# Right factors of the second and third token block made early and loaded at a block's end, and four left factors kept in HBM, in the ConvGLU half of a hybrid trunk kernel

## The chip, the cores and the metric

One core of a Trainium2 chip. The metric is the device time of one execution of the whole kernel in microseconds (us), with the median over the runs shown.

## What is computed

The reference is one layer of a streaming encoder trunk over 2048 frames of width 1024 (float32): an input projection, three token mixers, an output projection with a residual, and a convolutional GLU. The kernel returns the full layer (`out` is 1024 x 2048, transposed). Only the last two steps are touched here:

```
x = x + concat([ya, yb, yc]) @ w_out              # output projection
h = rms_norm(x, ffn_norm_g)
gate, val = split(h @ w_up)                       # w_up: 1024 x 5632
conv = conv_b + sum_i shift(gate, i) * conv_w[i]  # 3 taps along time
x = x + (silu(conv) * val) @ w_down               # w_down: 2816 x 1024
```

## The kernel before

**Precision.** Every matmul operand is a float32 split in a high and a low part (`split`: a cast on ACT, a subtraction on DVE), and every product is made of three matmuls (high x high, high x low, low x high).

**Token blocks.** Output projection and feed-forward go over three blocks of 688, 680 and 680 frames (`BL`), each taken as two halves of n = 344 or 340. In what follows they are the first, second and third block (b = 0, 1, 2 in the code).

**Output projection** (L1179 to L1237). For each block and each half hf it runs 8 k x 8 column tiles ct x 3 matmuls into all 8 PSUM banks. The mixers' output is loaded from HBM (`raw`), split into `yh` (5 buffers) and multiplied by `wo`. Then DVE adds each bank to the residual tile `Y` (L1224; one buffer per ct, loaded from the input for each block), the sum goes to HBM (`x2D`), and its squares are summed. The `stats` of a half (one matmul, Ln and Exp on ACT, giving `rsb`) are run two steps into the next half.

**Right factors.** The up projection uses a Strassen-like scheme: for a column tile fi of 128 of the 2816 hidden columns, 7 products instead of 8. The right factors `B0` to `B6` are made from the normalised block. `build` (L1151) does this in 4 steps j: two normalisations on DVE (L1157), four sums on POOL (L1162 to L1165), seven splits. That is 28 splits of 128 x n a block. The `B` tiles have one buffer each. The first block's factors are built in the output projection, while PE works on the second block's first half. Those of the second and third block are built at the end of the block before, beside the last two down projections (`PACE`).

**Left factors.** For each fi two raw tiles of w_up (512 KB each) are loaded (`up_w`); POOL makes four sums of their quarters (L1268 to L1271), and each of the 7 left factors is split into a `wu` tile (4 buffers) just before its product of 12 matmuls (L1282 to L1284). The products come in the order 0, 1, 6, 2, 3, 4, 5; those numbered 2 to 5 use the sums. All this is repeated for each of the three blocks.

**Down projection.** For each pair of fi, `ffn_down` runs 16 banks x 6 matmuls (L1328 to L1330), and DVE adds each bank to `acc` (L1331). Its weights `wd` are loaded raw and split by ACT and POOL (`down_w`). At a block's end two down projections follow each other, for fi 18, 19 and fi 20, 21. The second pair's weights are asked for after the first of them.

**Order.** The program is written as above, but a list scheduler sets the order on each engine, so rows of an engine can stand far from where they are written. All loads and stores of these stages are issued by one queue, SP, in order; a DMA that waits for a buffer holds up those behind it. The three `raw` buffers serve up and down weights alike.

## Time and profile before

| | |
|---|---|
| time, three runs | 3233.82 us median (3225.78 to 3234.05) |
| profiled execution | 3230.11 us, span 3228.3 us |
| PE busy | 3022.8 us, 94% of the span |
| DVE, ACT, POOL busy | 73%, 43%, 30% |
| output projection of the third block | about 1726.6 to 1787.5 us of the span |
| feed-forward | about 1787.5 to 3224.2 us of the span |

PE is the bound nearly everywhere, so a stretch is read by how many matmuls it starts: the steady feed-forward starts 633 in 100 us with n = 344 and 641 with n = 340, and a stretch that starts fewer has lost the difference. "PEclk" is the clock that TensorE was granted, as a share of 2.4 GHz; 1.00 is full speed and 0.5 would be 1.2 GHz throughout.

### The profile page before, as it was taken

What the parts mean: (1) busy time and instruction counts of PE and PEld (TensorE: products, weight loads), DVE (VectorE), ACT (ScalarE), POOL (GpSimd) and SP (SyncE); (2) the same over time, 40 slices, a digit from 0 to 9 for tenths busy, and PEclk for the clock granted to TensorE, in tenths of its full rate; (3) what the DMA queues carried; (4) which work ended last, traced back from release to release, by engine and by line L of the source; (5) the groups of instructions that cost most, each with busy time, mean ns of one, the idle gap of its engine ahead of it and who ended that gap; (6) DMA issues with size and microseconds to landing.
All of it is one profiled execution on the core that took longest, in us unless ns stands there. A gap on an engine that the chain in (4) does not pass through costs nothing.

```text
span 3228.3 us, 49120 instructions
## 1 busy us (share of the span) xinstructions
PE 3022.8 (94%) x17820; PEld 2638.5 (82%) x17820; DVE 2369.2 (73%) x4590; ACT 1397.6 (43%) x2610; POOL 952.5 (30%) x928
## 2 busy tenths in 40 slices
PE   6988999999999969999989899999899998999999
PEld 4666767777777745667789899998899998899998
DVE  6667676666767546677553788889988889888886
ACT  5434444544543325578532333334333334333332
POOL 1010020001000020144342444444444444444443
PEclk8998999999989979999999999999999999999999
DMA  7756655665634475422234422222422222422221
GB/s 221 210 158 180 200 164 149 182 172 166 173 109 126 141 175 150 127 73 82 77 98 154 134 79 79 77 68 79 157 79 79 79 78 82 134 74 79 79 79 68
DMA packets 310818, 392.92 MB, mean 122 GB/s; under 512 B 137144, under 2 KB 228804, under 8 KB 299752
## 3 DMA queue, kind: packets, MB, share of 16 engines
q1 hardware_dynamic: 305648, 377.99, 39.8%
q0 software_dynamic: 2816, 8.39, 0.9%
q10 hardware_dynamic: 2112, 3.41, 0.5%
q8 instruction: 141, 2.31, 0.3%
q14 instruction: 101, 0.83, 0.1%
HBM read 304.65 MB, written 86.36 MB: 121 GB/s over the span
## 4 chain that ended last, share of the span: by engine, by line
PE 66%; DVE 18%; issue 5%; DMA 4%; ACT 4%; POOL 2%; SPq 0%; POOLq 0%; ACTq 0%; DVEq 0%
PE ps L1284 7%; PE ps L1283 7%; PE ps L1282 7%; PE ps L1330 4%; PE ps L1328 4%; PE ps L1329 4%; PE mm L263 3%; PE mm L261 3%; PE mm L262 3%; PE o L1054 2%; DVE T L516 2%; DVE tm L513 2%; PE z L632 1%; PE ps L1190 1%; PE ps L1189 1%
## 5 line engine op out<-in xcount | busy, mean ns | idle before, releaser
L1284 PE MATMUL ps<-B,wu 128*128 128x340 f32 (+1 forms) x1848 | 593.4, 321 | 20.6 <-DVE wu L143 20.5
L1282 PE MATMUL ps<-B,wu 128*128 128x340 f32 (+1 forms) x1848 | 589.3, 319 | 3.5 <-ACT wu L142 2.4
L1283 PE MATMUL ps<-B,wu 128*128 128x340 f32 (+1 forms) x1848 | 591.8, 320 | 0.0
L1284 PEld LDWEIGHTS ps<-B,wu 128*128 128x128 f32 x1848 | 348.0, 188 | 28.1 <-DVE wu L143 27.7
L1328 PE MATMUL ps<-hid,wd 128*128 128x340 f32 (+1 forms) x1056 | 341.5, 323 | 14.3 <-ACT wd L142 10.2
L1282 PEld LDWEIGHTS ps<-B,wu 128*128 128x128 f32 x1848 | 347.9, 188 | 4.5 <-ACT wu L142 2.7
L1283 PEld LDWEIGHTS ps<-B,wu 128*128 128x128 f32 x1848 | 348.5, 189 | 0.3 <-DVE B L143 0.2
L1330 PE MATMUL ps<-hid,wd 128*128 128x340 f32 (+1 forms) x1056 | 339.6, 323 | 4.4 <-POOL wd L143 4.4
L1329 PE MATMUL ps<-hid,wd 128*128 128x340 f32 (+1 forms) x1056 | 339.6, 322 | 0.0
L261 PE MATMUL mm<-hT,w 128*128 128x512 f32 x704 | 312.6, 444 | 23.7 <-ACT w L142 15.3
L143 DVE TENSOR_TENSOR wu<-S,wu 128x512 fp32r<-128x512 f32 x264 | 256.2, 975 | 75.6 <-ACT wu L142 75.5
L262 PE MATMUL mm<-hT,w 128*128 128x512 f32 x704 | 289.6, 411 | 6.2 <-DVE hT L143 5.9
L263 PE MATMUL mm<-hT,w 128*128 128x512 f32 x704 | 289.4, 411 | 3.9 <-DVE w L143 3.8
L1331 DVE TENSOR_TENSOR acc<-acc,ps 128x340 f32<-128x340 f32 (+1 forms) x528 | 248.7, 505 | 52.8 <-PE ps L1330 51.6
L143 POOL TENSOR_TENSOR wd<-raw,wd 128x1024 fp32r<-128x1024 f32 x66 | 170.7, 2610 | 277.5 <-ACT wd L142 272.5
L142 ACT CAST wu<-S 128x512 fp32r<-128x512 f32 x264 | 163.1, 619 | 151.1 <-PE ps L1284 142.1
L1328 PEld LDWEIGHTS ps<-hid,wd 128*128 128x128 f32 x1056 | 201.2, 191 | 18.0 <-ACT wd L142 11.0
L143 DVE TENSOR_TENSOR wu<-raw,wu 128x512 fp32r<-128x512 f32 x198 | 203.3, 1028 | 5.6 <-ACT wu L142 5.6
L1330 PEld LDWEIGHTS ps<-hid,wd 128*128 128x128 f32 x1056 | 200.1, 190 | 6.6 <-POOL wd L143 6.6
L1329 PEld LDWEIGHTS ps<-hid,wd 128*128 128x128 f32 x1056 | 200.7, 190 | 0.0
L261 PEld LDWEIGHTS mm<-hT,w 128*128 128x128 f32 x704 | 137.8, 196 | 67.5 <-ACT w L142 16.7
L142 ACT CAST wu<-raw 128x512 fp32r<-128x512 f32 x198 | 121.5, 620 | 164.2 <-PE ps L1284 139.7
(335 smaller groups left out, 6816.4 us busy)
## 6 DMA issues: line engine op xcount, KB each, us to landing
w<-wD SPq DMA_DIRECT2D x72, 1024.0 KB
raw<-in_w_up_dram SPq DMA_DIRECT2D x132, 512.0 KB
raw<-in_w_down_dram SPq DMA_DIRECT2D x66, 512.0 KB
wD<-w SPq DMA_DIRECT2D x24, 1024.0 KB
wraw<-in_w_in_dram SPq DMA_DIRECT2D x24, 512.0 KB
xt<-in_xT_dram SPq DMA_DIRECT2D x48, 256.0 KB
K<-qkD SPq DMA_DIRECT2D x21, 512.0 KB
Q<-qkD SPq DMA_DIRECT2D x84, 128.0 KB
```

Source lines behind the costliest of these rows:

```text
L142: (hi_eng or nc.scalar).copy(hi, src) if (hi_eng or nc.scalar) is nc.scalar else hi_eng.tensor_copy(out=hi, in_=src)
L143: (lo_eng or nc.vector).tensor_tensor(lo, src, f(hi), op=ALU.subtract)
L261: mm(ps, hi[:, kt, 0:P], hT[kt][:, 0, :], start=(kt == 0), stop=False)
L262: mm(ps, hi[:, kt, 0:P], hT[kt][:, 1, :], start=False, stop=False)
L263: mm(ps, lo[:, kt, 0:P], hT[kt][:, 0, :], start=False, stop=(kt == KT - 1))
L1282: mm(ps, whl[:, 0, kt, :], Bs[p][:, kt, 0, 0:n], start=(kt == 0), stop=False)
L1283: mm(ps, whl[:, 0, kt, :], Bs[p][:, kt, 1, 0:n], start=False, stop=False)
L1284: mm(ps, whl[:, 1, kt, :], Bs[p][:, kt, 0, 0:n], start=False, stop=(kt == 3))
L1328: mm(ps, wd[:, 0, ch], hid[:, 0, cs], start=(u == 0), stop=False)
L1329: mm(ps, wd[:, 0, ch], hid[:, 1, cs], start=False, stop=False)
L1330: mm(ps, wd[:, 1, ch], hid[:, 0, cs], start=False, stop=(u == G - 1))
L1331: nc.vector.tensor_tensor(acc[ct][:, cs], acc[ct][:, cs], ps, op=ALU.add)
```

## The change

The names in the new code: `put(p, j, o)` is called for each of the 28 splits of a build. `direct` splits into the `B` tile as before; `stored` splits into a small `st` tile (two buffers) and writes it to HBM (`BD`).

- The second block's right factors are built and stored in the output projection, in the third block's first half.
- The third block's are built by `build_ahead(2)`, written in the second block's loop, and stored.
- At a block's end the 7 `B` tiles are loaded (1.4 MB each).
- In the first block, for fi > 1, each `wu` tile of the products 2 to 5 is also written to HBM (`kept`, 80 stores of 512 KB). The second and third block load them (160 loads) instead of making sums and splits, and load only half of the second raw tile.
- The last two down weights of a block are split ahead into four `wu` tiles (`down_last`). `wu` has 5 buffers instead of 4.
- The scratch for software DMA descriptors is cut from 8192 to 2048.

```
-    def build(Bs, b, src, tmp):
+    def build(put, b, src, tmp):
...
-                split(Bs[p][:, j, 0, 0:n], Bs[p][:, j, 1, 0:n], o)
+                put(p, j, o)
                 yield
...
+    def direct(Bs, n):
+        return lambda p, j, o: split(Bs[p][:, j, 0, 0:n], Bs[p][:, j, 1, 0:n], o)
+    later = {}
+    def stored(b):
+        n = BL[b][1]
+        later[b] = [dram.tile([P, 4, 2, n], F32, name=f"BD{b}{p}") for p in range(7)]
+        def put(p, j, o):
+            t = st4.tile([P, 2, HN], F32R, name="st")
+            split(t[:, 0, 0:n], t[:, 1, 0:n], o)
+            nc.sync.dma_start(out=later[b][p][:, j], in_=f(t[:, :, 0:n]))
+        return put
...
-                    if b == 1 and hf == 0:
-                        Bs = factors()
-                        work = build(Bs, 0, lambda kt, done=done: done[kt], tmp3)
+                    if hf == 0:
+                        if b == 1:
+                            Bs = factors()
+                        put = direct(Bs, BL[0][1]) if b == 1 else stored(1)
+                        work = build(put, b - 1, lambda kt, done=done: done[kt], tmp3)
...
+            k0 = 4 * part if (fi, 2) in kept and b else 0
+            nc.sync.dma_start(out=raw[:, k0:KT], in_=w_up[fi, part][:, k0:KT])
...
+            if left[p] is None:
+                nc.sync.dma_start(out=f(whl), in_=kept[fi, p])
+            else:
+                split(whl[:, 0], whl[:, 1], left[p])
+            if b == 0 and fi > 1 and 2 <= p <= 5:
+                kept[fi, p] = dram.tile([P, 2, 4, P], F32, name=f"wuD{fi}_{p}")
+                nc.sync.dma_start(out=kept[fi, p], in_=f(whl))
...
-        ready, work = [], iter(())
+        ready, work = [], build_ahead(2) if b == 1 else iter(())
...
+            for _ in itertools.islice(work, 2 if fi > 2 else 0):
+                pass
...
+        wdl = down_last(range(NF - G, NF))
         if b + 1 < len(BL):
...
             Bs = factors()
-            work = build(Bs, b + 1, load, tmp4)
+            for p in (0, 1, 6, 2, 3, 4, 5):
+                nc.sync.dma_start(out=f(Bs[p][:, :, :, 0 : BL[b + 1][1]]), in_=later[b + 1][p])
```

**DVE, third block's output projection.** The first fence is before: the last two `yh` splits of the first half, then the eight additions of its banks to Y0 to Y7, then the second half's splits.

```order
L143 TENSOR_TENSOR yh_16554<-raw_16552,yh_16554 128x340
L143 TENSOR_TENSOR yh_16591<-raw_16589,yh_16591 128x340
L1224 TENSOR_TENSOR Y0_16465<-Y0_16465,ps_16221 128x340
L1224 TENSOR_TENSOR Y1_16466<-Y1_16466,ps_16222 128x340
L1224 TENSOR_TENSOR Y2_16467<-Y2_16467,ps_16223 128x340
L1224 TENSOR_TENSOR Y3_16468<-Y3_16468,ps_16224 128x340
L1224 TENSOR_TENSOR Y4_16469<-Y4_16469,ps_16225 128x340
L1224 TENSOR_TENSOR Y5_16470<-Y5_16470,ps_16226 128x340
L1224 TENSOR_TENSOR Y6_16471<-Y6_16471,ps_16227 128x340
L1224 TENSOR_TENSOR Y7_16472<-Y7_16472,ps_16284 128x340
L143 TENSOR_TENSOR yh_16620<-raw_16618,yh_16620 128x340
L143 TENSOR_TENSOR yh_16649<-raw_16647,yh_16649 128x340
```

The second is the same engine in the changed kernel, at the end of the same stretch. `st` rows are splits of the second block's right factors.

```order
L143 TENSOR_TENSOR st_16527<-tmp_16440,st_16527 128x340
L143 TENSOR_TENSOR st_16541<-Y3_15891,st_16541 128x340
L1244 TENSOR_TENSOR Y6_16633<-Y6_16633,ps_16230 128x340
L143 TENSOR_TENSOR st_16545<-Y7_15895,st_16545 128x340
L143 TENSOR_TENSOR st_16549<-tmp_16534,st_16549 128x340
L1244 TENSOR_TENSOR Y3_16630<-Y3_16630,ps_16227 128x340
L143 TENSOR_TENSOR st_16553<-tmp_16535,st_16553 128x340
L143 TENSOR_TENSOR st_16586<-tmp_16533,st_16586 128x340
L143 TENSOR_TENSOR st_16590<-Y7_15895,st_16590 128x340
L143 TENSOR_TENSOR st_16594<-tmp_16536,st_16594 128x340
L1244 TENSOR_TENSOR Y7_16634<-Y7_16634,ps_16287 128x340
L143 TENSOR_TENSOR yh_16840<-raw_16838,yh_16840 128x340
```

The additions that free the first half's banks now stand among the 28 `st` splits: Y0 behind the ninth, Y7 behind the last.

**SP, first feed-forward block.** In the changed kernel these rows are from fi = 2 and 3 of the first block: `BD2x<-st` are stores of the third block's right factors, `wuD` stores of left factors, `raw<-in_w_up` the loads of coming weights.

```order
L1187 DMA BD22_21982<-st_22844 128x2x340
L1302 DMA raw_17764<-in_w_up_dram 128x1024
L1325 DMA wuD3_2_17679<-wu_17676 128x1024
L1325 DMA wuD3_3_17698<-wu_17695 128x1024
L1187 DMA BD23_21983<-st_22848 128x2x340
L1187 DMA BD24_21984<-st_23125 128x2x340
L1187 DMA BD25_21985<-st_23129 128x2x340
L1288 DMA x4_24130<-x2D_73 128x680
L1187 DMA BD26_21986<-st_23268 128x2x340
L1302 DMA raw_17766<-in_w_up_dram 128x1024
L1302 DMA raw_17919<-in_w_up_dram 128x1024
```

The scheduler has moved the whole third-block build, which is written in the second block's loop, into the first seven fi of the first block. Its 28 stores and its `x4` loads stand among the weights' loads.

**SP, end of the first block.** Before, from the raw tiles of the next block's fi = 1 (the two `in_w_up` rows) to the last load of `acc` (some rows of the same kind are not shown):

```order
L1264 DMA raw_21892<-in_w_up_dram 128x1024
L1264 DMA raw_21894<-in_w_up_dram 128x1024
L1316 DMA raw_21904<-in_w_down_dram 128x1024
L1374 DMA out_0_dram<-acc0_16830 128x688
L1374 DMA out_0_dram<-acc1_16831 128x688
L1374 DMA out_0_dram<-acc2_16832 128x688
L1339 DMA acc0_21741<-x2D_73 128x680
L1339 DMA acc1_21742<-x2D_73 128x680
L1374 DMA out_0_dram<-acc3_16833 128x688
L1374 DMA out_0_dram<-acc7_16837 128x688
L1339 DMA acc7_21748<-x2D_73 128x680
```

After, from the first `B` load (likewise):

```order
L1419 DMA B0_21686<-BD10_16294 128x8x340
L1419 DMA B1_21687<-BD11_16295 128x8x340
L1419 DMA B6_21692<-BD16_16300 128x8x340
L1419 DMA B5_21691<-BD15_16299 128x8x340
L1426 DMA out_0_dram<-acc0_16992 128x688
L1426 DMA out_0_dram<-acc7_16999 128x688
L1398 DMA acc0_21964<-x2D_73 128x680
L1398 DMA acc7_21971<-x2D_73 128x680
L1302 DMA raw_22122<-in_w_up_dram 128x1024
L1302 DMA raw_22124<-in_w_up_dram 128x1024
L1302 DMA raw_22279<-in_w_up_dram 128x1024
L1302 DMA raw_22281<-in_w_up_dram 128x512
```

The two raw tiles of the next block's fi = 1 stood ahead of the stores of `out` and the loads of `acc`; now they stand behind all sixteen.

## Rows read from the trace of the kernel before

**Rows 1.** The page: the span, PE's busy time, the clock granted in 40 slices, and two of the costliest groups (busy us, mean ns of one, idle time before them and its releaser).
```profile
span 3228.3 us, 49120 instructions
PE 3022.8 (94%) x17820; PEld 2638.5 (82%) x17820; DVE 2369.2 (73%) x4590; ACT 1397.6 (43%) x2610; POOL 952.5 (30%) x928
PEclk8998999999989979999999999999999999999999
L1284 PE MATMUL ps<-B,wu 128*128 128x340 f32 (+1 forms) x1848 | 593.4, 321 | 20.6 <-DVE wu L143 20.5
L1328 PE MATMUL ps<-hid,wd 128*128 128x340 f32 (+1 forms) x1056 | 341.5, 323 | 14.3 <-ACT wd L142 10.2
```

**Rows 2.** Stretches of the feed-forward. Columns: from and to, length; busy us of PE with the instructions started, the same for its weight loads, DVE, ACT, POOL; granted clock; DMA share; GB/s. Steady, end of the first block, steady, end of the second block, end of the kernel.
```profile
core 0: us, PE busy (x) PEld busy (x) DVE busy (x) ACT busy (x) POOL busy (x), PEclk, DMA share, GB/s
2000.00:2100.00 100.00, 100.00 (x633) 100.00 (x632) 87.29 (x128) 39.02 (x58) 45.16 (x35) 1.00 0.23 76
2200.00:2350.00 150.00, 133.35 (x797) 127.07 (x797) 139.66 (x193) 59.81 (x101) 74.38 (x59) 0.98 0.37 121
2400.00:2500.00 100.00, 100.00 (x641) 100.00 (x640) 88.12 (x128) 38.69 (x58) 43.97 (x35) 1.00 0.23 77
2700.00:2800.00 100.00, 85.74 (x502) 80.38 (x501) 93.36 (x132) 40.63 (x72) 52.14 (x43) 0.95 0.43 137
3200.00:3226.00 26.00, 21.32 (x124) 20.20 (x122) 10.73 (x22) 1.99 (x2) 4.70 (x2) 0.93 0.26 100
```

**Rows 3.** What PE waited for in the stretches 2200 to 2350 and 2700 to 2800: us in total, times, longest.
```profile
PE ps L1284 <- DVE wu L143: 7.5, 8, 2.6
PE ps L1328 <- ACT wd L142: 4.7, 1, 4.7
...
PE ps L1284 <- DVE wu L143: 6.5, 9, 1.2
PE ps L1328 <- ACT wd L142: 4.8, 1, 4.8
```

**Rows 4.** The build at the first block's end, 2200 to 2350: minimum, median and maximum ns of one split's halves on ACT and DVE, and of a normalisation on DVE.
```profile
L142 ACT CAST B<-u x16: 474/477/479, 2234.8 to 2277.7; 128x340 fp32r<-128x340 f32 x16
L143 DVE TENSOR_TENSOR B<-u,B x16: 500/598/2255, 2237.8 to 2282.4; 128x340 fp32r<-128x340 f32 x16
L1157 DVE SCALAR_TENSOR_TENSOR x<-x,pps,rsb x8: 914/920/1959, 2249.9 to 2306.9; 128x680 f32<-128x680 f32 x8
```

**Rows 5.** Output projection of the third block: the stretch (columns as in rows 2), the end of the statistics of the half before it on ACT, and the first additions of PSUM banks, of the half before it and of its first half, on DVE.
```profile
1725.00:1795.00 70.00, 70.00 (x448) 69.34 (x448) 25.27 (x46) 19.80 (x42) 21.24 (x21) 1.00 0.44 140
1737.44 0.49 ACT L1235 ACTIVATE rsb<-rsb 128x340 f32<-128x340 f32 x1
1726.56 3.73 DVE L1224 TENSOR_TENSOR Y<-Y,ps 128x340 f32<-128x340 f32 x8 [3.15 <-PE ps L1191]
1756.98 3.33 DVE L1224 TENSOR_TENSOR Y<-Y,ps 128x340 f32<-128x340 f32 x7 [3.17 <-PE ps L1191]
```

**Rows 6.** The first block's build in the output projection: the stretch, the end of the statistics and the first split's cast on ACT, then ns of one of the splits' halves and of one POOL sum.
```profile
1660.00:1710.00 50.00, 39.20 (x224) 37.41 (x223) 37.73 (x54) 22.38 (x50) 26.51 (x23) 0.90 0.39 113
1661.67 0.49 ACT L1235 ACTIVATE rsb<-rsb 128x344 f32<-128x344 f32 x1
1663.58 0.48 ACT L142 CAST B<-Y 128x344 fp32r<-128x344 f32 x1 [0.17 <-DVE Y L1157]
L142 ACT CAST B<-tmp x16: 477/479/483, 1665.6 to 1692.7; 128x344 fp32r<-128x344 f32 x16
L143 DVE TENSOR_TENSOR B<-tmp,B x16: 502/671/1241, 1667.4 to 1693.9; 128x344 fp32r<-128x344 f32 x16
L1163 POOL TENSOR_TENSOR tmp<-tmp,Y x4: 919/1250/1437, 1665.7 to 1689.3; 128x344 f32<-128x344 f32 x4
```

**Rows 7.** DMA times: two kinds of store from the POOL queue (KB each, us from issue to landing); the last store of the kernel, 340 KB, as SP issues it, and SP's wait for it after that; a 512 KB load as SP issues it (first of three) and the POOL sum that waits for it.
```profile
yD<-yl POOLq DMA_DIRECT2D x16, 256.0 KB, 3.7
yD<-yo POOLq DMA_DIRECT2D x32, 128.0 KB, 2.3
3224.78 0.33 SPq L1374 DMA_DIRECT2D out_dram<-acc  x1
SPq L1453 <- DMA out_dram<-acc: 1.8, 1, 1.8
1986.19 10.35 SPq L1264 DMA_DIRECT2D raw<-in_w_up_dram  x3
1989.76 1.61 POOL L1268 TENSOR_TENSOR S<-raw 128x512 f32<-128x512 f32 x1 [0.79 <-DMA raw<-in_w_up_dram]
```

**Rows 8.** The busiest stretch of the DMA engines in the output projection (columns as in rows 2).
```profile
1735.00:1745.00 10.00, 10.00 (x64) 9.67 (x63) 1.50 (x3) 2.46 (x5) 0.33 (x1) 1.00 0.98 337
```

**Rows 9.** The start of the feed-forward: the stretch, what PE waited for, and an ACT row that waits for a raw weight.
```profile
1787.50:1860.00 72.50, 64.10 (x388) 62.18 (x388) 61.27 (x89) 30.62 (x51) 32.73 (x24) 0.98 0.45 146
PE ps L1284 <- DVE wu L143: 6.0, 5, 1.8
PE ps L1282 <- ACT wu L142: 2.4, 1, 2.4
1797.97 1.05 ACT L142 CAST wd<-raw 128x1024 fp32r<-128x1024 f32 x1 [5.52 <-DMA raw<-in_w_down_dram]
```

**Rows 10.** Left factors in the first block's steady part, 1860 to 2200 (ns of one, minimum, median, maximum), and two POOL rows that stand one pair of fi apart.
```profile
L142 ACT CAST wu<-S x67: 602/621/627, 1859.9 to 2198.0; 128x512 fp32r<-128x512 f32 x67
L143 DVE TENSOR_TENSOR wu<-S,wu x67: 678/692/1942, 1860.5 to 2198.7; 128x512 fp32r<-128x512 f32 x67
1983.76 5.22 POOL L143 TENSOR_TENSOR wd<-raw,wd 128x1024 fp32r<-128x1024 f32 x2 [9.30 <-ACT wd L142]
2025.59 5.22 POOL L143 TENSOR_TENSOR wd<-raw,wd 128x1024 fp32r<-128x1024 f32 x2 [9.30 <-ACT wd L142]
```

**Rows 11.** What PE waited for in the kernel's last 25 us.
```profile
PE ps L1330 <- POOL wd L143: 2.2, 2, 1.1
PE ps L1328 <- ACT wd L142: 0.7, 1, 0.7
```

More of the change, by code (lines that the diff above doesn't have):

```diff
@@ L1263, in up_w @@
             raw = raw4([P, KT, P])
-            nc.sync.dma_start(out=raw, in_=w_up[fi, part])
+            k0 = 4 * part if (fi, 2) in kept and b else 0
+            nc.sync.dma_start(out=raw[:, k0:KT], in_=w_up[fi, part][:, k0:KT])
             raws.append(raw)
+        if b and (fi, 2) in kept:
+            return raws[0][:, 0:4], raws[0][:, 4:8], None, None, None, None, raws[1][:, 4:8]
         (a11, a12), (a21, a22) = ((r[:, 0:4], r[:, 4:8]) for r in raws)
@@ L1318, in down_w, with down_last @@
         split(wd[:, 0], wd[:, 1], raw, None, nc.gpsimd)
-        return wd
+        return lambda s, ct: wd[:, s, ct * P : (ct + 1) * P]
+    def down_last(fis):
+        raws = []
+        for fi in fis:
+            raw = raw4([P, DM])
+            nc.sync.dma_start(out=raw, in_=w_down[fi * P : (fi + 1) * P, :])
+            raws.append(raw)
+        whl = [[ws4.tile([P, 2, 4, P], F32R, name="wu") for _ in fis] for h in range(2)]
+        for u, raw in enumerate(raws):
+            for h in range(2):
+                t = whl[h][u]
+                split(t[:, 0], t[:, 1], raw[:, h * 512 : h * 512 + 512].rearrange("p (a c) -> p a c", c=P), None, nc.gpsimd)
+        return [lambda s, ct, u=u: whl[ct // 4][u][:, s, ct % 4, :] for u in range(len(fis))]
     def ffn_down(acc, grp, n):
         for ct in range(KT):
-            ch = slice(ct * P, (ct + 1) * P)
             for hf in range(2):
```

45 lines of the change are left out of this document (23 added, 22 removed).

## The prediction

> **What bounds the kernel now.** I read the page first: PE is busy for 3022.8 of 3228.3 us, and its clock is granted in full in nearly every slice of the feed-forward [rows 1]. Then I counted matmuls by stretch. The steady feed-forward starts 633 or 641 matmuls in 100 us, with PE at 100.00 [rows 2], which is 0.158 or 0.156 us each. There only PE's own work counts, and relief for DVE, ACT or POOL is worth nothing. The time that can be had lies where PE starts fewer:
> - End of the first block, 2200 to 2350: 797 matmuls, where about 955 would fit (150 us at the mean of the two rates). 158 x 0.157 = 24.8 us are lost [rows 2].
> - End of the second block, 2700 to 2800: 502 where 641 would fit. 139 x 0.156 = 21.7 us are lost [rows 2].
> - End of the kernel: the last 26 us hold 124. PE's work ends some 2 us before the stretch does, so 24.2 us could hold 155, and 31 x 0.156 = 4.8 us are lost [rows 2].
> - Start of the feed-forward, 1787.5 to 1860: 388 where 459 would fit at the first rate. 71 x 0.158 = 11.2 us are lost [rows 9, 2].
>
> The waits at the block ends say what it is: PE waits for left-factor splits on DVE (7.5 and 6.5 us) and for the down weights' cast on ACT (4.7 and 4.8 us) [rows 3], while DVE is busy for 139.66 of 150 us [rows 2]. What the waits do not explain is the clock, 0.98 and 0.95 there [rows 2].
>
> **The sum, term by term.** It is made against the profiled execution, 3230.1 us, which lies 3.7 under the median of the runs.
>
> *Block ends.* The 28 splits, 8 normalisations and 16 POOL sums go [rows 4], and the last down weights are split earlier, so both named waits lose their cause: 24.8 + 21.7 = 46.5 us can come back. In their place 7 x 1.39 = 9.75 MB of factors are loaded for each block. At 337 GB/s, the rate of the busiest stretch of the projection [rows 8], that is 29 us. The loads can start when the last up projection has used B0. Six of its products and two down projections are left, 6 x 12 + 2 x 96 = 264 matmuls, 41 us, which hide them. What may be late is the raw pair for fi = 1, which now stands behind 8 stores and 8 loads of 340 KB. The stores of out end with the last down projection; 2.8 MB of acc loads at 337 GB/s take 8.3 us after it, and 1 MB of raw 3.1 us, with about 2 us of latency. That is 13 us into the next block, and its second up projection starts 7 x 12 x 0.156 = 13.1 us into it, with a split of 1.3 us ahead of it [rows 10]. So between 0 and 6 us are lost at each of two ends. I take 1.5 each: **-43.5** (-46 to -35).
>
> *End of the kernel.* The waits there are for the last down weights [rows 11], which are now split beside the down projection before: **-4.3** (-4.8 to 0).
>
> *Output projection of the third block.* This is the price. Call s the start of the bank additions of the half before, 1726.6. Now the third block's first half ends at s + 30.4 (1756.98), and the second at s + 61 [rows 5]. PE has no gap there, DVE is busy for 25 of 70 us [rows 5], so the work has room. But the 28 splits go through two st tiles, and the additions that free the banks stand among them on DVE, the last behind the 28th. The second half needs these banks. The statistics are ready at s + 11.4 [rows 5], and in the first block's build the first split follows 1.4 us behind them [rows 6]: s + 12.8. An st tile is taken for a cast (0.48), a subtraction (0.5 to 0.67, rows beside it in [rows 6]), some 0.2 of hand-over, and the store. Two tiles overlap, so the interval is x = (1.25 + store) / 2. The trace has no such store from SP. Nearest: the last store of out, same size, 0.33 us of issue and 1.8 of wait, 2.1 us on an idle queue; 256 KB from POOL's queue takes 3.7 [rows 7]. That gives x between 1.68 and 2.48 us. I take 1.8, near the store of the same size and queue, a little longer because Y loads share the SP queue, and the next Y load waits for POOL to be done with the old Y. The last split ends at s + 12.8 + 27 x 1.8 + 1 = s + 62.4. Behind it come 2 us of addition and statistics, 15 matmuls of the last bank and the 72 of k = 5 to 7 (yh has five tiles, so they wait), 87 x 0.157 = 13.7 us: s + 78 to 80, against s + 61. With 2 us of lower clock, as in the stretch of the first block's build (0.90) [rows 6]: **+21**. Each 0.1 us of x is worth 2.7 us. The ends are +18 (x = 1.68) and +39 (x = 2.48). If the stores cost nothing, the splits go at the pace of that first build, 1.1 us each [rows 6], the last ends at s + 44, and the loss is 0 to 2.
>
> The Trainium skill ("DMA: Bandwidth & Descriptors", section "Anatomy of one DMA — SWDGE (gpsimd) path") gives about 2.0 us fixed plus bytes at 436 GB/s for a DMA, most of the fixed part being the receipt of the write, heaviest in HBM. It is written for another queue than SP's; by it 340 KB would take 2.8 us as an estimate, x would be 2.03, this term +27 and the whole sum 6 us worse. The row of the same size says 2.1 us [rows 7], and I stay with the row.
>
> *Start of the feed-forward.* The third block's build, 28 splits, 8 normalisations and 16 sums, falls into the first seven fi. One fi is half of 41.83 us [rows 10], so there are 146 us, of which DVE has 13 to 18% free [rows 2], 19 to 26 us. It gets 28 x 0.55 + 8 x 0.92 = 23 us [rows 4]. In the mean it fits; in bursts it won't, and a left-factor split on DVE can take 1.9 us instead of 0.69 [rows 10]. I charge 10 us. Against it, the second half of the projection is late, so the first raw tiles are there in time, and of the 11.2 us lost now (8.4 in waits for first left factors, with ACT held 5.5 us by a raw down weight) [rows 9] I give back 4. Net **+6** (-5 to +20).
>
> *Steady blocks.* 80 stores and 160 loads of 512 KB, 42 and 84 MB, lie beside a queue that moves 76 GB/s [rows 2] and has shown 337 [rows 8]. A 512 KB load takes 3.6 us from issue to use [rows 7], and a wu tile is free for more than that in a ring of five products of 1.9 us each. The sums and splits saved have no price, since PE is full. **+1** (0 to +10). The smaller descriptor scratch and the fifth wu buffer: 0.
>
> Sum: -43.5 - 4.3 + 21 + 6 + 1 = -19.8, so 3210 from the profiled execution and 3214 from the median. Forecast: **3212 us**.
>
> **Rivals.**
> 1. *The price is dearer, the gain is eaten.* A store as slow as the POOL queue's 3.7 us gives +39 instead of +21 [rows 7]; or the start costs its upper end, +20, because SP holds stores of st behind loads that wait for a raw buffer, and ACT then waits for an st tile with left factors behind it. Either leaves -2 to -6: 3224 to 3240. For it: st has two tiles. Against: the same-size store takes 2.1.
> 2. *Slower.* The same st ring, with one mechanism: a store lands late because the Y load ahead of it on SP waits for POOL. The other terms give -40.8, so the balance is at x = 2.53 us, and it is slower by more than 9.7 us from x = 2.9, a store that lands 4.5 us after its split. At 5 us x is 3.1 and the time 3245. Against: only 8 of 28 stores have a Y load ahead of them.
> 3. *The stores are hidden.* If landing takes 1 us or less, or the additions get by earlier, the projection costs 2 instead of 21 and the time is about 3193. Against: the shortest store that the trace shows is 2.1 us [rows 7].
> 4. *The block ends don't come back,* because the loads of B are late. At half of 337 GB/s they would take 58 us against 41 and give back 15 of 22 us at each end: about 3240. Against: the other traffic there is some 76 GB/s [rows 2].
>
> **How the numbers follow.** A change under 0.3% (9.7 us) can't be told from none. The forecast's case, 3201 to 3224, has 0.50; rival 1, with rival 4 in its reach, 0.23; rival 2 0.14; rival 3 0.13. So faster 0.63, same 0.23, slower 0.14. The range takes in most of rivals 1 and 3: 3194 to 3243.
>
> **What would show it.** At both block ends matmuls at 64 in 10 us, DVE well under full, no wait for ACT wd. In the third block's projection a stretch in which PE stands for some 15 to 20 us, waiting for DVE's additions to Y, with `st` casts on ACT waiting for DMA, 1.7 to 2.0 us apart. In the first seven fi a few waits for DVE or ACT wu. I am wrong if st splits are over 2.5 us apart, if PE still waits at the block ends (for B, acc or raw), or if the steady blocks drop under 640 in 100 us in the loads of wu.

## The result: 37 us slower

The changed kernel takes 3270.61 us (median of 4 runs, 3254.61 to 3278.11) against 3233.48 us before (median of 4 runs, one more than the three above): 1.0114 times as long (95% interval 1.0072 to 1.0155). The forecast was 3212 us with a range up to 3243, so it missed in size and in sign. The profiled execution is the fastest of the four, 3254.6 us with a span of 3252.7 us, 24.4 us above the span before.

PE takes the same matmuls in nearly the same order in both kernels. So the time of a stage can be read from the starts of its first matmul and of the next stage's. This table is worked out from these starts in the two traces, in us. The feed-forward has 8712 matmuls, 2904 a block. The first 1848 of a block are as many as seven pairs of fi have, each with its two up projections and one down projection.

```
stage (in matmuls)                        before   after   change   forecast
up to the third block's projection        1729.6  1729.3    -0.3
third block's projection                    61.0   102.5   +41.5      +21
feed-forward, first block: first 1848      304.4   323.2   +18.8       +6
    its last 1056                          182.4   167.3   -15.1  |
second block: first 264                     51.0    49.4    -1.6  |  -43.5
    its last 2640                          428.4   413.2   -15.2  |
third block: first 264                      48.9    50.5    +1.6  |
    its last 2640, to the end              422.5   417.2    -5.3       -4.3
```

The gain at the block ends is there, though smaller than forecast: 30.3 us. Two prices, 41.5 and 18.8 us, eat it twice over. The forecast sum was -19.8 (with +1 for the steady blocks, which has no row here), the measured one is +24.4. Of these 44 us the projection makes 20.5, the start of the feed-forward 12.8, and the block ends with the starts of the blocks behind them 13.2.

The page after, as [rows 1]: the span, the engines, and one of PE's groups with the idle time ahead of it.

```profile
span 3252.7 us, 49359 instructions
PE 3028.6 (93%) x17820; PEld 2647.1 (81%) x17820; DVE 2159.4 (66%) x4430; ACT 1305.7 (40%) x2456; POOL 701.4 (22%) x774
...
L1387 PE MATMUL ps<-hid,wd 128*128 128x340 f32 (+1 forms) x960 | 307.8, 321 | 3.6 <-DVE acc L1390 2.4
```

PE's wait for `ACT wd`, 10.2 us at L1328 before, is gone from the same matmuls after (L1387). PE now waits elsewhere. Stretches after, as [rows 2, 5, 9] (matmuls in brackets after PE's busy time, then the other engines; at the end the granted clock, DMA share and GB/s):

```profile
1750.00:1775.00 25.00, 19.13 (x111) 18.32 (x109) 11.26 (x22) 7.44 (x16) 6.83 (x7) 0.93 0.84 247
1775.00:1800.00 25.00, 12.73 (x48) 11.59 (x49) 7.75 (x14) 6.47 (x14) 5.19 (x7) 0.65 0.77 220
1800.00:1825.00 25.00, 15.48 (x68) 14.20 (x67) 5.40 (x10) 7.28 (x15) 5.86 (x8) 0.67 0.45 150
1850.00:2000.00 150.00, 130.32 (x763) 124.95 (x762) 133.61 (x189) 60.02 (x102) 75.72 (x59) 0.95 0.64 221
2000.00:2100.00 100.00, 100.00 (x633) 100.00 (x632) 83.07 (x129) 40.38 (x61) 52.46 (x34) 1.00 0.54 184
2300.00:2400.00 100.00, 94.32 (x588) 93.05 (x587) 67.55 (x110) 27.84 (x42) 21.33 (x18) 0.98 0.68 245
2750.00:2850.00 100.00, 94.57 (x584) 93.08 (x583) 71.24 (x112) 27.34 (x42) 20.64 (x19) 0.97 0.69 241
3226.00:3252.00 26.00, 22.90 (x147) 22.62 (x146) 13.20 (x27) 0.00 (x0) 0.00 (x0) 1.00 0.28 108
```

Three stretches of 25 us in the projection start 111, 48 and 68 matmuls where about 160 fit. From 1850 to 2000, in the first block's early fi, 763 start where 950 fit. The steady rate is back at 2000 (633). The two stretches with a block's end and the start of the next have 588 and 584 where 641 fit.

What PE waited for in the projection, from 1735 to 1830, and what ACT waited for (us in total, times, longest):

```profile
PE ps L1207 <- DVE Y L1244: 18.1, 6, 9.0
PE ps L1253 <- POOL rsb L1249: 8.9, 1, 8.9
...
ACT st L142 <- DMA BD<-st: 34.7, 20, 3.0
```

ACT's casts into `st` wait 34.7 us for earlier stores to land. PE waits for the additions to Y, which stand behind these splits, and at the end of the stretch 8.9 us for the statistics. The chain of work that ended last in this stretch names the stores (start, us from issue to landing):

```profile
1759.77 3.91 DMA BD<-st
...
1778.80 4.93 DMA BD<-st
...
1801.82 2.66 DMA BD<-st
```

Eight such pieces between 1758 and 1804 have a mean of 3.55 us. The 28 splits on DVE start between 1739.40 and 1806.23: 2.48 us apart in the mean.

In the first fi of the feed-forward, from 1850 to 2000 (PE, then ACT):

```profile
PE ps L1330 <- DVE wu L143: 11.0, 7, 2.6
...
ACT st L142 <- DMA BD<-st: 55.1, 18, 7.1
```

DVE's time for the 28 splits and 8 normalisations of a build (busy us, mean ns of one), first where the changed kernel runs the third block's, 1850 to 2010, then in the kernel before, at the first block's end, 2200 to 2350:

```profile
L143 DVE TENSOR_TENSOR st<-t,st 128x340 fp32r<-128x340 f32 x16 | 15.8, 986 | 5.5 <-ACT st L142 5.4
L143 DVE TENSOR_TENSOR st<-x,st 128x340 fp32r<-128x340 f32 x12 | 9.8, 817 | 4.3 <-ACT st L142 4.3
L1158 DVE SCALAR_TENSOR_TENSOR x<-x,pps,rsb 128x680 f32<-128x680 f32 x8 | 11.1, 1390 | 1.3 <-DMA x<-x2D 1.2
...
L143 DVE TENSOR_TENSOR B<-u,B 128x340 fp32r<-128x340 f32 x16 | 11.9, 748 | 2.7 <-ACT B L142 2.7
L143 DVE TENSOR_TENSOR B<-x,B 128x340 fp32r<-128x340 f32 x12 | 12.8, 1073 | 0.0
L1157 DVE SCALAR_TENSOR_TENSOR x<-x,pps,rsb 128x680 f32<-128x680 f32 x8 | 9.3, 1178 | 0.0
```

That is 36.7 us after and 34.0 before, where the forecast has 23.

And at the first block's end: PE's waits between 2290 and 2420, SP's issues in order (start, us in all, count), and the first cast of the next block's fi = 1:

```profile
PE ps L1328 <- ACT wu L142: 3.0, 1, 3.0
PE ps L1330 <- DVE wu L143: 2.2, 2, 1.4
...
2294.89 16.19 SPq L1419 DMA_DIRECT2D B<-BD  x6
2311.18 12.27 SPq L1426 DMA_DIRECT2D out_dram<-acc  x8
2323.50 6.13 SPq L1398 DMA_DIRECT2D acc<-x2D  x8
2329.99 1.72 SPq L1302 DMA_DIRECT2D raw<-in_w_up_dram  x2
...
2337.97 1.89 ACT L142 CAST wu<-raw 128x512 fp32r<-128x512 f32 x3 [0.74 <-DMA raw<-in_w_up_dram]
```

B, out, acc and the raw pair come in the order that the changed kernel's schedule gave them. The pair is issued between 2329.99 and 2331.7, and ACT gets the first tile at 2337.97, 8 us after its issue, behind 2.8 MB of acc loads and 15.6 us into the second block.

### The profile page after: what moved, and what is told of

Same layout as the page of the kernel before. It is cut to its first block, busy times and chain, and to the rows that moved or that the text cites. A ratio compares the mean times of both kernels' runs of the same rounds, so it can differ in the third digit from the quotient of the medians.

```text
span 3252.7 us, 49359 instructions
## 1 busy us (share of the span) xinstructions
PE 3028.6 (93%) x17820; PEld 2647.1 (81%) x17820; DVE 2159.4 (66%) x4430; ACT 1305.7 (40%) x2456; POOL 701.4 (22%) x774
## 4 chain that ended last, share of the span: by engine, by line
PE 67%; DVE 15%; DMA 7%; ACT 4%; issue 4%; POOL 2%; SPq 0%; ACTq 0%; DVEq 0%; POOLq 0%
PE ps L1329 8%; PE ps L1330 8%; PE ps L1328 8%; PE ps L1387 5%; PE ps L1388 5%; PE ps L1389 5%; PE mm L263 3%; PE mm L261 3%; PE mm L262 3%; PE o L1054 2%; DMA BD<-st 2%; DVE T L516 2%; DVE tm L513 2%; PE z L632 2%; PE st L1036 1%
## 5 line engine op out<-in xcount | busy, mean ns | idle before, releaser
L1328 PE MATMUL ps<-B,wu 128*128 128x340 f32 (+1 forms) x1848 | 592.8, 321 | 10.7 <-ACT wu L142 9.0
L1328 PEld LDWEIGHTS ps<-B,wu 128*128 128x128 f32 x1848 | 350.3, 190 | 12.8 <-ACT wu L142 10.5
L1390 DVE TENSOR_TENSOR acc<-acc,ps 128x340 f32<-128x340 f32 (+1 forms) x528 | 256.6, 505 | 108.6 <-PE ps L1389 108.6
L1387 PE MATMUL ps<-hid,wd 128*128 128x340 f32 (+1 forms) x960 | 307.8, 321 | 3.6 <-DVE acc L1390 2.4
L1388 PE MATMUL ps<-hid,wd 128*128 128x340 f32 (+1 forms) x960 | 306.7, 319 | 1.2 <-DVE hid L143 1.2
L1389 PE MATMUL ps<-hid,wd 128*128 128x340 f32 (+1 forms) x960 | 306.7, 319 | 0.0
L143 POOL TENSOR_TENSOR wd<-raw,wd 128x1024 fp32r<-128x1024 f32 x60 | 148.7, 2499 | 289.1 <-ACT wd L142 288.5
L143 DVE TENSOR_TENSOR wu<-raw,wu 128x512 fp32r<-128x512 f32 x198 | 163.9, 830 | 48.0 <-ACT wu L142 42.6
L261 PEld LDWEIGHTS mm<-hT,w 128*128 128x128 f32 x704 | 138.4, 197 | 66.5 <-ACT w L142 16.9
L1387 PEld LDWEIGHTS ps<-hid,wd 128*128 128x128 f32 x960 | 181.1, 189 | 5.7 <-DVE acc L1390 3.6
L1388 PEld LDWEIGHTS ps<-hid,wd 128*128 128x128 f32 x960 | 180.5, 188 | 1.5 <-DVE hid L143 1.5
L1389 PEld LDWEIGHTS ps<-hid,wd 128*128 128x128 f32 x960 | 180.6, 188 | 0.0
L262 PEld LDWEIGHTS mm<-hT,w 128*128 128x128 f32 x704 | 138.3, 196 | 45.4 <-issue 10.3
L263 PEld LDWEIGHTS mm<-hT,w 128*128 128x128 f32 x704 | 137.8, 196 | 37.8 <-DVE w L143 6.9
```

What stands on the lines that cost most here:

```text
L143: (lo_eng or nc.vector).tensor_tensor(lo, src, f(hi), op=ALU.subtract)
L261: mm(ps, hi[:, kt, 0:P], hT[kt][:, 0, :], start=(kt == 0), stop=False)
L262: mm(ps, hi[:, kt, 0:P], hT[kt][:, 1, :], start=False, stop=False)
L263: mm(ps, lo[:, kt, 0:P], hT[kt][:, 0, :], start=False, stop=(kt == KT - 1))
L1328: mm(ps, whl[:, 0, kt, :], Bs[p][:, kt, 0, 0:n], start=(kt == 0), stop=False)
L1387: mm(ps, wd(0, ct), hid[:, 0, cs], start=(u == 0), stop=False)
```

## The experiments

Each is compared with runs of the kernel before on the same chip, whose medians were 3236.3 to 3236.4 us. Stage times are those of each kernel's own profile, by the method of the table above. Where the code is the same, a stage differs mostly by under 1 us between profiles, but the projection with its stores has 102.5 to 106.6 us and the first 1848 matmuls beside the third block's build 323.2 to 326.6. The start of the third block's projection differs by up to 14 us between profiles of kernels that are the same up to there, so stages are compared, not spans.

**1. One piece for each partition in st.**

```
-            t = st4.tile([P, 2, HN], F32R, name="st")
+            t = st4.tile([P, 2 * HN], F32R, name="st")[:, 0 : 2 * n].rearrange("p (s c) -> p s c", s=2)
```

> The changed kernel, with one edit: the st tile holds its two parts side by side, so that each partition's 2720 bytes are one piece in SBUF as they are in HBM (before: two pieces of 1360). Theory A (a store lands 3.7 us after its split because it is cut into twice as many pieces as the 340 KB store of out, which took 2.1 us): the ACT casts into st come about 1.7 to 1.8 us apart instead of 2.48, the third block's projection is some 18 us shorter, and the start of the feed-forward some us. Theory B (the stores are late because of the other traffic in the queue or the writing itself): casts 2.4 to 2.5 us apart, time within 5 us of the changed kernel.

Measured: 1.0097 (1.0065 to 1.0128). Splits 2.28 us apart, the projection 96.8 us (102.5 in the changed kernel), the first 1848 matmuls 324.8. The size of the pieces is worth some 6 us, a third of what theory A asked for. B is nearer.

**2. Five st tiles in the projection.**

```
+    def stored(b, ring=(None,)):
+        ring = itertools.cycle(ring)
...
+            pool = next(ring) or st4
+            t = pool.tile([P, 2, HN], F32R, name="st", bufs=2 if pool is st4 else 3)
...
-                        put = direct(Bs, BL[0][1]) if b == 1 else stored(1)
+                        put = direct(Bs, BL[0][1]) if b == 1 else stored(1, (st4, y3, y3, st4, y3))
```

> The changed kernel, with five st tiles instead of two in the third block's projection alone (two as before in the feed-forward). Theory A (what costs is the latency of a store, seen through a ring of two): the splits run at the pace of the direct build, 1.1 to 1.3 us apart, the projection gives back 30 to 38 of the 40 us that it lost, about 3235 us. Theory B (what costs is the DMA rate: 28 stores, the Y loads, the mixers' output and x2D are about 18 MB, 54 us at 337 GB/s): the splits come 1.7 to 2.0 us apart and 10 to 20 us come back. The start of the feed-forward stays as it is, some 29 us of PE lost between 1850 and 2000, by both.

Measured: 1.0063 (1.0039 to 1.0086). The splits come 1.33 us apart, as theory A said: latency through a ring of two set the pace, since the same DMA engines move a store every 1.33 us when five may be under way. But theory A's time did not come: the projection still takes 96.8 us. SP's rows (start, us, count) and PE's longest wait say why:

```profile
1750.66 32.30 SPq L1189 DMA_DIRECT2D BD<-st  x27
1783.05 4.50 SPq L1242 DMA_DIRECT2D Y<-in_xT_dram  x7
1788.36 6.84 SPq L1247 DMA_DIRECT2D x2D<-Y  x8
1795.25 9.14 SPq L1216 DMA_DIRECT2D raw<-yD  x8
...
PE ps L1209 <- ACT yh L142: 29.1, 1, 29.1
```

SP now issues 27 stores in a row, then seven Y loads, then the stores of x2D, then the second half's inputs, and PE stands for 29.1 us until the first of those is split. The Y tiles have one buffer, so the additions that free the banks can't run before the build has read the old Y. The ring was one link of the chain, and this order is the next.

**3. Third block's factors built at the second block's end, as before the change.**

```
-        ready, work = [], build_ahead(2) if b == 1 else iter(())
+        ready, work = [], iter(())
...
+            if b + 1 == 2:
...
+                work = build(direct(Bs, n1), b + 1, load, tmp4)
```

> The changed kernel, but the third block's right factors are built at the second block's end straight into the B tiles, as before the change; the rest stays. Theory A (the third block's build, moved by the scheduler into the first fi of the first block, costs some 18 us there because ACT stands waiting for st tiles with the left factors' casts behind it): the start loses about 11 us instead of 29, as before, and the second block's end loses about 20 instead of 9: net 5 to 10 us faster than the changed kernel. Theory B (the start suffers from the stores of left factors and the late end of the projection, not from that build): the start stays at 25 to 30 us and the kernel gets about 10 us slower.

Measured: 1.0059 (1.0038 to 1.0079). The first 1848 matmuls take 301.0 us instead of 323.2, and the second block's last 2640 take 420.9 instead of 413.2. The build costs 22 us where the scheduler put it, and saves 8 where it was taken from. (The projection, the same code as in the changed kernel, took 106.6 us here against 102.5.) The stores of left factors cost nothing here: experiment 12, which has none, also takes 301.0 for the first 1848.

**4. Both builds inside the running feed-forward, held back by the conv carry.** Each `st` tile first gets a tiny copy from `gcar`, the last two columns that the convolution of an fi carries to the next block. So its split can't be moved ahead of that fi.

```
             t = st4.tile([P, 2, HN], F32R, name="st")
+            nc.gpsimd.tensor_copy(out=f(t[:, 0, 0:2]), in_=gcar[:, now[0], :])
             split(t[:, 0, 0:n], t[:, 1, 0:n], o)
...
-                        put = direct(Bs, BL[0][1]) if b == 1 else stored(1)
-                        work = build(put, b - 1, lambda kt, done=done: done[kt], tmp3)
+                        work = build(direct(Bs, BL[0][1]), 0, lambda kt, done=done: done[kt], tmp3)
...
-        ready, work = [], build_ahead(2) if b == 1 else iter(())
+        ready, work = [], build_ahead(b + 1) if b < 2 else iter(())
...
+            now[0] = fi
```

> The changed kernel, but no right factors are stored in the projection: those of the second block are built from x2D in the first feed-forward block and those of the third in the second block, two splits for each fi from fi = 3 on. A tiny POOL copy from the conv carry of that fi into each st tile keeps the scheduler from moving them up. Theory A (the whole loss is in the two places where the builds were put, and the block ends' gain of 29 us stands): projection and start as before the change, no new waits in the blocks, about 3197 us in its own profile and 3200 to 3205 in the median. Theory B (what costs is DVE and ACT work and DMA traffic added to a full feed-forward, wherever it is put): the first block starts fewer than 630 matmuls in 100 us throughout and the time stays above 3225.

Measured: 0.9994 (0.9972 to 1.0016). The projection is back at 62.1 us, but the first 1848 matmuls take 324.1 us, as many as with the clustered build, and the second block's last 2640 take 418.8 instead of 413.2. Spreading the splits did not make them cheaper: theory A failed for the first block, in this form at least (experiment 11 takes it up). The time, 3234.38 us, is theory B's.

**5. The left factors and the last weights alone.** Both builds stand at the block ends as before the change.

> The changed kernel without any stored right factors: the second and the third block's are built at the block ends as before the change. What is left of the change is the four kept left factors, the last down weights split ahead and the fifth wu buffer. Theory A (these parts are a gain by themselves, since the relief of DVE and ACT at the block ends is theirs, and stores and loads of wu cost nothing): the feed-forward's first 1848 matmuls take 301 us (before the change 304.4), the second block's last 2640 take 421 (428.4), the kernel's end gives 5 us; together some 20 to 25 us faster than before, about 3212. Theory B (wu loads and stores eat what they save): within 5 us of before.

Measured: 0.9973 (0.9955 to 0.9990). First 1848: 300.4; second block's last 2640: 420.8; as expected by stages, though the median gained 10 us and not 20.

**6. The third block's build in the second block.** As experiment 5, with `build_ahead(2)` in the second block, held by the carry of the fi before (`gcar[:, now[0] - 1, :]`).

> As the run with both builds at the block ends, but the third block's right factors are built and stored in the second feed-forward block, two splits for each fi, held to that place by a tiny POOL copy from the conv carry of the fi before, and loaded at the second block's end. The second block's are built at the first block's end as before the change. Theory A (DVE has room only in the second block, where the kept left factors have taken work off it): the second block's last 2640 matmuls take 413 to 417 us instead of 421, so 3 to 8 us faster than that run. Theory B (a split in a running block costs about what it saves at the end, wherever it stands): no difference between the two runs.

Measured: 0.9940 (0.9921 to 0.9959). The second block's last 2640 matmuls take 413.4 us, the full rate, as theory A said. There the build is free. In this block the kept left factors have brought DVE down from 88 us in 100 [rows 2] to 66 with this build included, and POOL from 44 to 18 (197.10 and 53.41 of 300 in the second stretch of experiment 11). Which of the two it needs was not tested.

**7. The build's DVE and POOL work alone.** As experiment 3, with a build at the changed kernel's place whose `put` is only

```
+            nc.vector.tensor_tensor(t[:, 1, 0:n1], o, o, op=ALU.subtract)
```

> A measurement of one cost. The kernel with the third block's factors built at the second block's end (second block's stored in the projection) gets extra work at the place where the changed kernel builds the third block's: the same eight loads and normalisations, the same sixteen POOL sums and 28 DVE subtractions of the same size, but no ACT casts and no stores; the results are thrown away. Theory A (DVE and POOL have no room in the first feed-forward block): its first 1848 matmuls take 315 to 323 us, as in the changed kernel (323.2), against 301 without the extra work. Theory B (ACT, which waits in order for st tiles, and the stores are the cost): 301 to 306 us.

Measured, in one execution: the first 1848 matmuls take 319.0 us, 18 of the 22 us. In the stretch (columns as above) DVE is busy for 153 of 160 us, and PE waits for left factors on DVE and for a hidden tile:

```profile
1850.00:2010.00 160.00, 144.97 (x848) 140.07 (x847) 153.26 (x215) 56.48 (x86) 85.02 (x63) 0.95 0.53 182
...
PE ps L1344 <- DVE wu L143: 10.0, 10, 3.0
PE ps L1402 <- DVE hid L143: 2.3, 1, 2.3
```

With no cast and no store in it, the build costs nearly as much: theory A's range. So the work on DVE and POOL (with its eight loads) is enough for 18 of the 22 us, and the casts and stores add some 4 to it. What they would cost alone, with ACT's 55.1 us of waiting for st, was not run, nor was DVE's part tested apart from POOL's.

**8. Raw tiles of fi = 1 through ACT's queue.** As experiment 6, with this edit for the second and third block:

```
-            nc.sync.dma_start(out=raw[:, k0:KT], in_=w_up[fi, part][:, k0:KT])
+            (nc.scalar if b and fi == 1 else nc.sync).dma_start(out=raw[:, k0:KT], in_=w_up[fi, part][:, k0:KT])
```

> As the run with the third block's build in the second block, but the two raw tiles of fi = 1 of the second and third block are loaded through ACT's queue instead of SP's, so that they don't stand behind the stores of out and the loads of acc. Theory A (these late raw tiles cost the 8 to 9 us that the first 264 matmuls of a block lose): those take 43 to 46 us instead of 50, 4 to 12 us faster in all. Theory B (the loss is DVE's and POOL's share of the first fi, or the DMA engines are full, so another queue changes nothing): 49 to 51 us.

Measured: 0.9924 (0.9904 to 0.9944). The third block's first 264 matmuls take 41.7 us instead of 50.5, the full rate (264 x 0.1565 = 41.3). PE's only wait there, the two issues on ACT's queue, and SP's acc loads, behind which they no longer stand:

```profile
PE ps L1329 <- DMA wu<-wuD: 0.2, 1, 0.2
...
2725.91 0.33 ACTq L1303 DMA_DIRECT2D raw<-in_w_up_dram  x1
2743.55 0.33 ACTq L1303 DMA_DIRECT2D raw<-in_w_up_dram  x1
...
2751.24 5.12 SPq L1399 DMA_DIRECT2D acc<-x2D  x8
```

The second block, whose factors are still built at the block end here, keeps its 54.3 us (55.1 in experiment 6). There PE waits for DVE, so the raw pair is not the only cause that can slow a block's start.

**9. The projection's stores on ACT's queue, two st tiles.**

```
-            nc.sync.dma_start(out=later[b][p][:, j], in_=f(t[:, :, 0:n]))
+            q.dma_start(out=later[b][p][:, j], in_=f(t[:, :, 0:n]))
...
-                        put = direct(Bs, BL[0][1]) if b == 1 else stored(1)
+                        put = direct(Bs, BL[0][1]) if b == 1 else stored(1, nc.scalar)
```

> The changed kernel, with the 28 stores of the third block's projection issued by ACT's queue instead of SP's; still two st tiles. Theory A (a store takes 3 to 4 us to land by itself, from any queue): an ACT cast into st every 2.2 to 2.5 us, the projection of the third block 95 to 103 us (102.5 in the changed kernel, 61.0 before the change). Theory B (the stores stand on SP behind loads of Y that wait for POOL): the casts come 1.7 to 1.9 us apart, the projection takes 80 to 88 us.

Measured: splits 2.76 us apart, projection 108.9 us, one execution of 3266.12 us. ACT's waits and two of the stores (start, us to landing):

```profile
ACT st L142 <- DMA BD<-st: 42.0, 17, 4.2
...
1758.18 6.15 DMA BD<-st
...
1799.60 2.88 DMA BD<-st
```

Ten such stores between 1758 and 1812 take 2.6 to 6.2 us, 4.1 in the mean. A store is no faster from another queue. The loads of Y that stand ahead on SP were not what made it late.

**10. Five st tiles and ACT's queue together,** with experiments 6 and 8.

> The second block's factors stored in the projection as in the changed kernel, but through five st tiles and ACT's queue, so that SP is free for Y and for the mixers' output; the third block's built in the second feed-forward block as in the run with the third block's build there; raw tiles of fi = 1 through ACT's queue. Theory A (with the ring and the queue out of the way, only the order Y free, Y loaded, bank added is left): splits 1.3 to 1.5 us apart, the projection takes 80 to 88 us instead of 102.5, the second block's start 42 to 44; about 3208 in its profile. Theory B (the DMA engines are the limit): the projection stays above 94 us and the time above 3215.

Measured: 0.9965 (0.9947 to 0.9984), splits 1.72 us apart, projection 97.5 us, with one wait of PE of 27.4 us for the second half's first split. The numbers are theory B's, but not for its reason: in experiment 2 the DMA engines had moved the same stores 1.33 us apart. On ACT the second half's casts (`yh`) stand behind the last st cast, so PE has no second half until the build is through:

```profile
1795.21 0.47 ACT L142 CAST st<-tmp 128x340 fp32r<-128x340 f32 x1 [1.08 <-DVE st L143]
1795.59 0.85 ACT L142 CAST yh<-raw 128x340 fp32r<-128x340 f32 x2
```

The second block's first 264 matmuls take 43.4 us.

**11. Both builds in the feed-forward, held by the fi before, and the raw tiles through ACT's queue.**

> The second block's factors built and stored in the first feed-forward block and the third's in the second, two splits for each fi, each held by the conv carry of the fi before (not of the same fi, as in the first paced run), and the raw tiles of fi = 1 through ACT's queue. Theory A (the first block has no room on DVE, so 23 us of DVE work cost it 18 to 20 us of PE wherever they stand): its first 1848 matmuls take 317 to 321 us; its end and the next block's start give back 25, so the time is within 6 us of the run with the second block's build at the block end and the ACT queue (3211). Theory B (most of that cost was waiting in order for the conv carry): 303 to 310 us, some 10 us faster than that run.

Measured: 3208.11 us, 0.9916 (0.9896 to 0.9937), the lowest median of the study, though the interval overlaps experiment 8's. The first 1848 matmuls take 313.8 us (300.7 in experiment 8), between the two theories. The next 1056 take 170.3, the two starts 42.6 and 41.8. Two stretches, of the first and of the second block, PE's waits in the first block, and DVE's splits into st in the first and then in the second block (busy us, mean ns of one):

```profile
1900.00:2200.00 300.00, 290.26 (x1821) 287.60 (x1820) 261.16 (x396) 119.26 (x190) 150.72 (x135) 1.00 0.63 208
2400.00:2700.00 300.00, 300.00 (x1917) 300.00 (x1917) 197.10 (x344) 92.58 (x141) 53.41 (x75) 1.00 0.58 198
...
PE ps L1389 <- DVE hid L143: 10.8, 7, 1.9
PE ps L1331 <- DVE wu L143: 6.0, 7, 1.7
...
L143 DVE TENSOR_TENSOR st<-t,st 128x340 fp32r<-128x340 f32 x16 | 16.4, 1025 | 9.4 <-ACT st L142 9.4
L143 DVE TENSOR_TENSOR st<-x,st 128x340 fp32r<-128x340 f32 x12 | 12.6, 1049 | 7.5 <-ACT st L142 5.4 <-DMA raw<-in_w_down_dram 2.1
...
L143 DVE TENSOR_TENSOR st<-t,st 128x340 fp32r<-128x340 f32 x16 | 10.1, 633 | 0.0
L143 DVE TENSOR_TENSOR st<-x,st 128x340 fp32r<-128x340 f32 x12 | 8.5, 708 | 0.0
```

With the hold one fi looser the price fell from 23 us (experiment 4) to 13: part of it had been the wait for the carry, as theory B said. The rest, with 3 us in the block's last 1056, stays in the first block, where PE waits for splits on DVE, and is absent in the second. The same 28 splits take 29.0 us of DVE in the first block and 18.6 in the second, where POOL, at 53.41 us of 300 instead of 150.72, is far less busy beside them. Whether POOL is what stretches them was not tested. Without this build DVE has 55 us of 300 free in the first block (experiment 8):

```profile
1900.00:2200.00 300.00, 300.00 (x1895) 300.00 (x1894) 245.00 (x375) 113.45 (x169) 142.17 (x98) 1.00 0.50 172
```

So here the build fits DVE's free time in the mean, and PE still pays 16 us.

**12. The last weights alone.** As experiment 5 without the kept left factors.

> Only the last down weights split ahead, the fifth wu buffer and the smaller scratch are left of the change: both builds at the block ends, no left factors kept. Theory A (the kept left factors give the gain at the block ends): the second block's last 2640 matmuls take 426 to 428 us, as before the change, and only the kernel's end gives 5 us. Theory B (the down weights' wait of 4.7 us and the end are all that the run with both builds at the ends has gained): 421 us there, the same time as that run.

Measured: 0.9992 (0.9976 to 1.0007). The second block's last 2640 matmuls take 425.3 us (428.4 before, 420.8 with the kept factors), its first 264 take 57.0 (52.1). So the kept left factors are worth some 5 us in each of these. What this kernel keeps gains 3 us at a block's end, but the next block's start loses 6 (57.0 against 51.0 before). There one raw tile of the pair stands behind out and acc here too and is issued only 11.6 us into the block, without any loads of B.

## Why the prediction was wrong, point by point

**The projection: the mechanism was right, its size was not.** The chain was the one forecast: casts wait for stores, additions for casts, PE for additions. The step that failed is the value of x, the time from one split to the next. I took 1.8 us, by the store of out of the same size on a quiet queue (2.1 us), and measured is 2.48, the upper end that the POOL queue's 3.7 us gave [rows 7]. The landing was 3.55 us in the mean. That is 27 x 0.68 = 18 us. The second, smaller miss is the tail: I gave 2 us to the last addition and the statistics. The last Y load was issued only at 1806.02, the addition ran at 1810.15 and PE's matmul for the statistics at 1812.32; from the end of the last split to there are 5.6 us, and to the first matmul behind it 7.7. Against these 24 us stands a slip the other way: the forecast set its end, s + 78 to 80 with all matmuls in it, against s + 61. But before the change the feed-forward's first matmul starts at 1790.6, which is s + 64, so by its own terms the forecast was +18 and not +21. With the 24 that makes 42, and 41.5 were measured. The Trainium skill's rule ("DMA: Bandwidth & Descriptors", section "Anatomy of one DMA — SWDGE (gpsimd) path"), written for the gpsimd path and not for SP's, has about 2.0 us fixed plus the bytes at 436 GB/s, which gives an estimate of 2.8 us for such a store. This case's trace does not agree with it, with a mean of 3.55 us, but the estimate was nearer than the 2.1 us of the row that I preferred.

**The start of the feed-forward: right place, wrong price.** I charged 10 us and gave 4 back. A gain of 3.4 is there (301.0 against 304.4 in experiment 3), but not by the reason given, a late second half of the projection: experiments 5 and 12, whose projection is as fast as before, have it too (300.4 and 301.0). That size was luck. The price is 22, and DVE and POOL work alone is enough for 18 of these (experiment 7). The step that failed is "in the mean it fits": 23 us of work in 19 to 26 us of free time. The free time was right (25.05 of 160 us between 1850 and 2010 in experiment 3), the work was not: the 28 splits and 8 normalisations took 36.7 us. The forecast had charged 0.55 us a split, below the median of [rows 4], where the trace of before has means of 0.75 and 1.07, 34.0 us in all. And room in the mean is not enough either, as experiment 11 shows. That PE needs a split at a certain moment, so that DVE's idle time elsewhere doesn't help, fits PE's waits there, but was not tested by itself. Rival 1 had the right sum here, +20, by ACT held at st. ACT is held, 55.1 us, but experiment 7 comes within 4 us of the price without that.

**The block ends: both named waits went, a third stayed.** Block by block the last matmuls run at the full rate (1056 x 0.158 = 167), as forecast, 15 us each. But 9.7 and 7.6 of the 46.5 us that I had counted were lost in the next block's first 264 matmuls (51.0 and 48.9 against 41.3), and these stayed: 49.4 and 50.5. Here too the mechanism was named, the raw pair behind 16 DMAs, with 0 to 6 us at each end and 1.5 chosen. It was 8 to 9: the first tile was there 15.6 us into the second block and not 13. PE waits 5.7 and 5.4 us in the two starts, and the rest of the loss stands beside a lower clock (0.98 and 0.97 in the stretches). Experiment 8 moves that pair alone, and the third block's loss is gone; the second block's 264 matmuls take 43.4 and 42.6 us where its factors are loaded as in the changed kernel and the pair goes through ACT's queue (experiments 10 and 11). PE still waiting at the block ends for raw was one of the forecast's own signs of being wrong, and the one that came. Another, splits over 2.5 us apart, just failed to come at 2.48.

**What held.** The end of the kernel (-5.3 for -4.3). The steady blocks: 413.2 us for 2640 matmuls in the second block, so its 80 loads of 512 KB cost nothing, and the first block's 80 stores cost nothing either (301.0 us with them in experiment 3 and without them in experiment 12). The loads of B were hidden; rival 4 fell.

**The rivals.** Rival 2 named the cause "a store lands late because a Y load ahead of it on SP waits". Experiment 9 takes that away and nothing gets faster. So rival 2 had the right sign, through the ring, but the wrong reason. Its balance at x = 2.53 was reckoned with the other terms as forecast. With those as they came, x = 2.48 was enough.

**What stays open.** The stage table explains 24.4 us, the difference of the two profiled executions. The medians differ by 37.1. The other three executions of the changed kernel (3267.5, 3273.7, 3278.1) had lower mean granted clocks, 0.957 to 0.953 against 0.962, but where in the program they lost the time was not seen. Nor was it settled why these stores land later than the last store of out; their size in pieces is a small part (experiment 1), the issuing queue none (experiment 9). The other traffic is left as a rival: the DMA engines are busy for 0.84 and 0.77 of two of the projection's stretches, and for 0.26 at the end of the kernel before [rows 2]. No run took it away. What made the first 1848 matmuls 3 us faster without the build is open too: before has one profile, and the fifth wu buffer is common to the runs that are faster.

## What to carry to other kernels

A store into HBM that gives a small ring its buffers back was a latency here, not a bandwidth: price it by the slow end of the rows, and ask what stands on the same engine behind the waiting instruction. Work for an engine that is at 84% beside a full TensorE was dear in the first block: 22 us of PE for a build of 36.7 us on DVE in one place, and still 16 where it was spread out. Price such work by the mean of the rows and not by their low end, and put it where the engine has been relieved (here the second block, where it cost nothing). When a boundary is changed, look up what is now last in the queue: two raw tiles behind sixteen DMAs cost 8 to 9 us at each of two block starts, over half of the 15 us gained at the end before.

## What the runs showed of the hardware

A store of 340 KB from the st tiles took 2.7 to 4.9 us from issue to landing in the changed kernel, and 2.6 to 6.2 from ACT's queue in experiment 9, whereas the kernel's last store of out had taken 2.1 before the change. The same split of 128x340 on DVE took 1.04 us in the mean in the first block of experiment 11 and 0.66 in the second. With PE waiting up to 9.0 us at a time between bursts of matmuls, the granted clock of TensorE fell to 0.65 and 0.67 over two stretches of 25 us, between its levels of 1.2 and 2.4 GHz (0.5 and 1.00). That made the projection dearer than the waits alone: its last 87 matmuls, from 1814.46 on, took 17.4 us, where 87 x 0.157 = 13.7.
